# Gating projection of a hybrid encoder layer: x transposed by the host, inner dimension outermost

## The chip, the cores and the metric

The kernel runs on one core of a Trainium2 chip. Its time is the device time of one launch in microseconds; "before" is the median of three runs. A trace of one execution, taken by the profiler, shows what each engine did and when. The engines are TensorE (PE; its weight loads are listed as PEld), VectorE (DVE), ScalarE (ACT), GpSimd (POOL) and SyncE (SP), which here only issues transfers.

## The reference

One layer on x of 1024 rows (sequence) by 1024 columns, all in float32. The change is in its first part:

```python
h = rms_norm(x, norm_mix[l])
proj = h @ w_in[l]                       # 1024 x 2304 columns
z_sgu, z_s5, z_qkv = jnp.split(proj, [2 * SGU_WIDTH, 2 * SGU_WIDTH + S5_WIDTH], axis=-1)
o_a = sgu_mixer(jax.nn.gelu(z_sgu), ...) # 512 columns: u * (w @ rms_norm(v) + b), blocks of 128 rows
o_b = s5_mixer(z_s5, ...)                # 256 columns: a diagonal state-space scan, GELU, GLU
o_c = band_attention(q, k, v, ...)       # 3 x 512 columns: 8 heads, each chunk of 64 sees 9 chunks
x = x + group_rms(concat[o_a, o_b, o_c]) @ w_out[l]
x = x + moe(rms_norm(x))                 # 16 experts, two of one group for each row
```

`sgu_mixer` is called the gating unit here, and the product that gives its 512 columns the gating projection.

## The kernel before

**Precision.** Each large product of float32 operands is made of three matmuls (`mm3`, L129): both operands are split into a high part in a shorter format and a low part that holds the rest (`split`, L125: ScalarE writes the high part, VectorE the low one), and high times high, high times low and low times high are added up in one PSUM bank. A matmul has at most 512 columns here.

**Norm and projections.** The RMS norm's gain `gmix` is folded into the transposed x; its row factor `rs` is applied when a projection's result is copied out of PSUM. For each of four pairs of 128-row tiles of x (loop `pr`, L199), TensorE transposes the pair's 16 squares of 128x128 into PSUM (`hTp`, L205), ScalarE writes the high part `hT` scaled by the gain (L209), VectorE the low part `lT` (L210). ScalarE also squares the rows of x with a sum (L218), from which a short chain of VectorE steps makes `rs` for the pair. Then `sgu_proj` (L190) runs the gating projection of the pair's two tiles: all eight slices of the inner dimension (k) by three matmuls into one bank, and a GELU scaled by `rs` into `gz`.

**What follows.** S5's projection (L439 on, 96 matmuls, result transposed in `zT`), then k's, q's and v's (`qk_proj`, L608, and the loop at L855), eight tiles each of 24 matmuls. Attention, the output product, the router and the experts come after.

**Side work.** The gating unit (`sgu`, L249, six steps) and S5 (`s5`, L459, 21 steps) are generators in a list `side`. `tick(n)` (L90) draws n steps of the first one that isn't finished. The ticks stand beside the projections' tiles: two for each of the four tiles of S5's projection, which use up the gating unit's steps, then one for each tile of k, q and v, for S5's.

```python
    def tick(n=1):
        while n and side:
            try:
                next(side[0])
                n -= 1
            except StopIteration:
                side.pop(0)
```

**Order.** Up to attention, the order in which each engine (and each queue of transfers) gets its instructions isn't written out: a planner simulates the program and gives each engine, whenever it is free in that simulation, the ready instruction that stands earliest in the program. On the chip each engine then works strictly in that order. Attention, output and experts have an order written by hand.

**Memory.** PSUM has eight banks: three buffers of two banks with the tag `big`, and two of one bank with the tag `acc`. In SBUF there are 16 buffers of 4 KB per partition with the tag `slot`, 12 more with the tag `far` (the names in `FAR`, L28, among them `xt`, `bc_in`, `wsr`, `vn`, `vh`), and four with the tag `raw` for weights as they arrive. A tile that finds no free buffer waits until an earlier one is no longer read.

**Transfers.** x and the large weights are loaded by SyncE's queue. The small parameters (`gains`, the gating unit's `row256`, `sgb` and `wsr`, S5's `lam`, `ldt`, `bc_in` and `d5`, and `gqk`, from which VectorE makes `gq` at L635) are loaded by ScalarE's queue.

Of the kernel before, what the change touches and what calls it, by code (L numbers as in the profile page):

```python
# [4 lines left out]
F32 = mybir.dt.float32  # L5
F32R = mybir.dt.float32r
BF = mybir.dt.bfloat16
# [24 lines left out]
def trunk(tc, A, dbg=None, upto="all"):  # L32
# [35 lines left out]
    def slot(name, shape, dt=F32, far=None):  # L68
        far = name in FAR if far is None else far
        return slots.tile(shape, dt, name=name, tag="far" if far else "slot", bufs=FARS if far else SLOTS)  # L70
# [4 lines left out]
    def big(name, shape, dt=F32):  # L75
        return psum.tile(shape, dt, name=name, tag="big", bufs=3)

    def acc(name, shape, dt=F32):
        return psum.tile(shape, dt, name=name, tag="acc", bufs=2)
# [19 lines left out]
    def f32(ap):  # L99
        return ap.bitcast(F32)  # L100
# [37 lines left out]
    def load_x(tb):  # L138
        t = slot("xt", [128, D])
        sp.dma_start(t, x[tb * 128:(tb + 1) * 128, :])  # L140
        return t
# [6 lines left out]
    def junk():  # L148
        return work.tile([128, D], BF, name="junk", tag="w2")
# [17 lines left out]
    def load_w(c0, n, far=()):  # L167

        his, los = [], []
        per = 1024 // n  # L170
        for r in range(KD // per):
            rw = raw("rw", [128, per, n])
            sp.dma_start(rw, w_in[r * per * 128:(r + 1) * per * 128, c0:c0 + n]
                         .rearrange("(k p) c -> p k c", p=128))
            h = slot("wh", [128, per, n], F32R, far=r in far)
            l = slot("wl", [128, per, n], F32R, far=r in far)
            split(h, l, rw)
            his += [h[:, i] for i in range(per)]
            los += [l[:, i] for i in range(per)]
        return his, los  # L180

    def proj(out, sel, w, ks=range(KD)):
        his, los = w
        for k in ks:
            mm3(out, hT[k][:, sel], lT[k][:, sel], his[k], los[k], k == ks[0], k == ks[-1])

    gz = []
    rs = const("rs", [128, NT])

    def sgu_proj(tb):  # L190
        a = acc("pj", [128, 512])
        proj(a, slice(tb * 128, (tb + 1) * 128), W["sgu"])
        if tb % 2 == 0:
            gz.append(slot("gz", [128, 2, 512]))
        act.activation(gz[tb // 2][:, tb % 2], a, AF.Gelu_apprx_tanh, scale=rs[:, tb:tb + 1])

    W = {}
    xs = {0: load_x(0), 1: load_x(1)}
    for pr in range(4):  # L199
        for kq in range(2):  # L200
            p = big("hTp", [128, 4, 256])
            for q in range(2):
                for k in range(4):
                    kk = 4 * kq + k
                    pe.transpose(p[:, k, q * 128:(q + 1) * 128], xs[2 * pr + q][:, kk * 128:(kk + 1) * 128], ident)  # L205
            for k in range(4):
                kk = 4 * kq + k
                sl = slice(pr * 256, (pr + 1) * 256)
                act.activation(hT[kk][:, sl], p[:, k], AF.Copy, scale=gmix[:, kk:kk + 1])  # L209
                dve.scalar_tensor_tensor(lT[kk][:, sl], p[:, k], gmix[:, kk:kk + 1], f32(hT[kk][:, sl]),  # L210
                                         op0=OP.mult, op1=OP.subtract)
        if pr == 0:
            W["sgu"] = load_w(0, 512)
            for tb in range(2, NT):
                xs[tb] = load_x(tb)
        ss = small.tile([128, 2], F32, name="ssx")
        for q in range(2):
            act.activation(junk(), xs[2 * pr + q], AF.Square, accum_out=ss[:, q:q + 1])  # L218
        rsqrt(rs[:, 2 * pr:2 * pr + 2], ss, 2, 1.0 / D)
        if pr == 3:  # L220
            W["s5"] = load_w(512, 256)
        sgu_proj(2 * pr)
        sgu_proj(2 * pr + 1)
    W["k"] = load_w(1280, 512)

    div8, mod8 = const("div8", [128, 16]), const("mod8", [128, 8])
# [10 lines left out]
    row256 = const("row256", [128, 256])  # L237
    gsgu, glub = row256, row256
    wsr = slot("wsr", [128, 4, 128])
    act.dma_start(gsgu, bass.AP(tensor=A["sgu_norm"].tensor, offset=A["sgu_norm"].offset, ap=[[0, 128], [1, 256]]))  # L240
    sgb = const("sgb", [128, 4])
    act.dma_start(sgb, A["sgu_bT"])
    act.dma_start(wsr, A["sgu_wT"])
    pool.memset(wsr[64:128, :, 0:64], 0.0)
    wsh = slot("wsh", [128, 2, 4, 128], F32R)
    split(wsh[:, 0], wsh[:, 1], wsr)
# [58 lines left out]
            v = v.rearrange("p (a b c) -> p a b c", a=shape[1], b=shape[2])  # L305
        return v

    lam = const("lam", [128, 2, NG])
    act.dma_start(lam, A["lam2"])
    ldt = const("ldt", [128, NG])  # L310
    act.dma_start(ldt, bass.AP(tensor=A["log_dt"].tensor, offset=A["log_dt"].offset, ap=[[0, 128], [1, NG]]))
    bc_in = slot("bc_in", [128, 4, NG, 16])
    act.dma_start(bc_in, A["bc2"])
    d5 = const("d5", [16, NG])
    act.dma_start(d5, A["s5_dT"])
    dt = const("dt5", [128, NG])
    act.activation(dt, ldt, AF.Exp)
    th = const("th5", [128, NG])
# [120 lines left out]
    for i in range(2):  # L439
        for ts in (slice(0, 512), slice(512, S)):  # L440
            a = acc("pj", [128, 512])
            his, los = W["s5"]
            for k in range(KD):
                wk, wl_ = (t[:, i * 128:(i + 1) * 128] for t in (his[k], los[k]))
                mm3(a, wk, wl_, hT[k][:, ts], lT[k][:, ts], k == 0, k == KD - 1)
            act.activation(zT[i][:, ts], a, AF.Copy)
            tick(2)
    for i in range(2):
        p = big("s5z", [128, 8, 128])
        for j in range(8):  # L450
# [157 lines left out]
    def qk_proj(name, w):  # L608
        out = []
        for tb in range(NT):  # L610
            a = acc("pj", [128, 512])
            proj(a, slice(tb * 128, (tb + 1) * 128), w)
            if tb % 2 == 0:
                out.append(slot(name, [128, 2, 512]))
                s16 = small.tile([128, 2, 8], F32, name="s16")
                r16 = small.tile([128, 2, 8], F32, name="r16")
            act.activation(out[-1][:, tb % 2], a, AF.Copy, scale=rs[:, tb:tb + 1])
            sq = work.tile([128, 512], F32, name="sqk", tag="w2")
            act.activation(sq, a, AF.Square, scale=rs[:, tb:tb + 1])
            dve.tensor_reduce(s16[:, tb % 2], sq.rearrange("p (h c) -> p h c", c=64), axis=AX.X, op=OP.add)  # L620
            if tb % 2 == 1:
                rsqrt(r16.rearrange("p a b -> p (a b)"), s16.rearrange("p a b -> p (a b)"), 16, 1.0 / 64)
                ov = out[-1].rearrange("p t (h c) -> p t h c", c=64)
                dve.tensor_tensor(ov, ov, bc(r16[:, :, :, None], [128, 2, 8, 64]), op=OP.mult)
            tick(1)
        return out

    kt_ = qk_proj("kt", W["k"])
    W["q"] = load_w(768, 512, (0, 1))
    qt_ = qk_proj("qt", W["q"])  # L630
    W["v"] = load_w(1792, 512, (3,))
    gqk = const("gqk", [128, 2])
    act.dma_start(gqk, A["qk2"])
    gq = const("gq", [128, 1])
    dve.scalar_tensor_tensor(gq, gqk[:, 0:1], 64 ** -0.5, gqk[:, 1:2], op0=OP.mult, op1=OP.mult)  # L635

# [969 lines left out]
def layout(inputs):  # L1606

    import numpy as np
    i = {k: np.asarray(v) for k, v in inputs.items()}
    f = np.ascontiguousarray  # L1610
    o = {"x": i["x"], "w_in": i["w_in"][0]}
    lr, li = i["s5_lambda_re"][0].T, i["s5_lambda_im"][0].T
    o["lam2"] = np.stack([np.concatenate([lr, lr]), np.concatenate([li, li])], 1)
    br, bi = (i[n][0].transpose(1, 0, 2) for n in ("s5_b_re", "s5_b_im"))
    cr, ci = (i[n][0].transpose(2, 0, 1) for n in ("s5_c_re", "s5_c_im"))
    o["bc2"] = np.stack([np.concatenate(p) for p in ((br, bi), (bi, br), (cr, ci), (ci, cr))], 1)
    o["log_dt"] = i["s5_log_dt"][0]
    o["s5_dT"] = i["s5_d"][0].reshape(16, 16).T
    o["glu_w"] = i["s5_glu_w"][0]
    o["glu_b"] = i["s5_glu_b"][0]  # L1620
    o["sgu_norm"] = i["sgu_norm"][0]
    o["sgu_bT"] = i["sgu_b"][0].T
    o["sgu_wT"] = i["sgu_w"][0].transpose(2, 0, 1)
    o["qk2"] = np.stack([np.concatenate([i[n][0]] * 2) for n in ("q_norm", "k_norm")], 1)
    o["norm_ffn"] = i["norm_ffn"][0]
    o["gT"] = np.stack([i[n][0].reshape(8, 128).T for n in ("norm_mix", "out_norm", "norm_ffn")], 1)
    o["w_out"] = i["w_out"][0]
    o["w_router"] = np.concatenate([i["router_group_w"][0], i["router_expert_w"][0].transpose(1, 0, 2).reshape(D, 16)], 1)
    o["b_router"] = np.concatenate([i["router_group_b"][0], i["router_expert_b"][0].reshape(16)])
    o["w_gu"] = np.concatenate([i["w_gate"][0], i["w_up"][0]], 2)  # L1630
    o["w_down"] = i["w_down"][0]
    rb = i["rel_bias"][0]
    rx = np.concatenate([np.repeat(rb[:, 512:], 639 - 255, axis=1), rb[:, 129:512][:, ::-1]], axis=1)

    o["relT"] = np.stack([rx[:, 127 - q:767 - q] for q in range(128)], 1)
    return {k: f(v) for k, v in o.items()}
# [17 lines left out]
```

## Time and profile before

| | |
|---|---|
| median of 3 runs | 825.13 us (822.68 to 826.71) |
| the profiled execution, its own time | 823.16 us |
| its span, first to last instruction | 821.4 us |
| mean granted TensorE clock | 0.980 of full speed |
| TensorE, VectorE, ScalarE, GpSimd busy | 91%, 65%, 49%, 25% |
| front: gating projection up to | 66.2 us |
| S5's projection up to, about | 90.7 us |
| k's, q's and v's projections up to, about | 268 us |
| attention up to, about | 410 us |

The span is what the trace covers; the execution's own time is 1.8 us longer. Busy time counts matmuls that overlap in the pipeline once. The granted clock is the share of full speed that TensorE was given; its two levels are 1.2 and 2.4 GHz.

### The profile page before, as it was taken

How to read it: one execution, taken by the hardware profiler on the slowest of the kernel's cores; microseconds unless marked ns; L12 is line 12 of the kernel's file. 1: busy time of each engine (PE TensorE's matmuls, PEld its weight loads, DVE VectorE, ACT ScalarE, POOL GpSimd, SP SyncE). 2: the span in 40 equal slices, each digit the busy share in tenths (PEclk: the TensorE clock that was granted, in tenths of full speed). 3: DMA queues.
4: the chain of work that ended last, by engine and by line, in shares of the span. 5: the costliest groups of instructions: out<-in, count | busy, mean ns of one | idle time of the engine just before them, and what ended most of it. 6: DMA issues, size and time to landing. Idle time of an engine off the chain costs nothing. (4 is left out here: it accounts for less than half of the span.)

```text
span 821.4 us, 13661 instructions
## 1 busy us (share of the span) xinstructions
PE 749.3 (91%) x5024; PEld 635.3 (77%) x5025; DVE 533.7 (65%) x1266; ACT 401.9 (49%) x752; POOL 202.9 (25%) x235
## 2 busy tenths in 40 slices
PE   5999999899999777899988999958899999999995
PEld 3878788788888667888876888737778788888884
DVE  4875769968534568777965544768675774575541
ACT  6763342312444677777864333423554553464441
POOL 0000224423132431213001211112332353242221
PEclk9999999999999999999999999989999999999998
DMA  8423011222000410001055233385989999899663
GB/s 310 146 57 103 7 15 15 72 46 41 14 1 1 128 28 1 2 26 53 2 186 203 104 120 112 121 293 176 337 263 273 337 351 305 212 310 308 129 156 55
DMA packets 56516, 111.31 MB, mean 136 GB/s; under 512 B 24272, under 2 KB 28880, under 8 KB 56432
## 3 DMA queue, kind: packets, MB, share of 16 engines
q1 hardware_dynamic: 46880, 84.14, 30.6%
q0 software_dynamic: 6480, 23.60, 12.1%
q10 hardware_dynamic: 3072, 2.49, 1.0%
q8 instruction: 47, 0.77, 0.4%
q14 instruction: 37, 0.30, 0.1%
HBM read 90.05 MB, written 20.17 MB: 134 GB/s over the span
## 5 line engine op out<-in xcount | busy, mean ns | idle before, releaser
L130 PE MATMUL pj<-wh,hTh 128*128 128x512 f32 x256 | 103.8, 406 | 0.8 <-ACT hTh L209 0.7
L131 PE MATMUL pj<-wl,hTh 128*128 128x512 f32 x256 | 102.0, 399 | 2.5 <-DVE wl L127 2.4
L132 PE MATMUL pj<-wh,hTl 128*128 128x512 f32 x256 | 100.8, 399 | 0.5 <-DVE hTl L210 0.4
L130 PE MATMUL gup<-gh,hgh 128*128 128x256 f32 x304 | 89.9, 296 | 1.7 <-PEq L1581 0.3
L132 PE MATMUL gup<-gh,hgl 128*128 128x256 f32 x304 | 87.0, 286 | 3.0 <-DVE hgl L1282 3.0
L1325 PE MATMUL yp<-rwd,hh 128*128 128x256 f32 (+1 forms) x264 | 86.1, 465 | 0.0
L131 PE MATMUL gup<-gl,hgh 128*128 128x256 f32 x304 | 86.1, 283 | 0.0
L977 DVE TENSOR_TENSOR gl<-rwg,gh 128x1024 fp32r<-128x1024 f32 x64 | 78.4, 1247 | 6.9 <-ACT gh L972 6.6
L1325 PEld LDWEIGHTS yp<-rwd,hh 128*128 128x128 f32 x264 | 46.8, 194 | 23.7 <-issue 17.8
L972 ACT ACTIVATE gh<-rwg 128x1024 fp32r<-128x1024 f32 x64 | 64.1, 1052 | 1.1 <-DMA rwg<-in_w_gu 0.2
L130 PEld LDWEIGHTS gup<-gh,hgh 128*128 128x128 f32 x304 | 58.1, 191 | 6.1 <-ACT y L1334 5.2
L132 PEld LDWEIGHTS gup<-gh,hgl 128*128 128x128 f32 x304 | 58.1, 191 | 4.4 <-DVE hgl L1282 3.5
L131 PEld LDWEIGHTS pj<-wl,hTh 128*128 128x128 f32 x256 | 48.7, 190 | 13.6 <-DVE wl L127 3.3
L132 PEld LDWEIGHTS pj<-wh,hTl 128*128 128x128 f32 x256 | 48.5, 190 | 13.1 <-DVE hTl L210 1.6
L130 PEld LDWEIGHTS pj<-wh,hTh 128*128 128x128 f32 x256 | 48.6, 190 | 12.9 <-ACT hTh L209 2.4
L131 PEld LDWEIGHTS gup<-gl,hgh 128*128 128x128 f32 x304 | 58.2, 192 | 0.1
L1337 POOL DMA_INDIRECT out<-y,ix x22 | 38.0, 1729 | 80.9 <-ACT y L1334 44.9
L127 DVE TENSOR_TENSOR ptl<-ps,pth 128x640 fp32r<-128x640 f32 (+2 forms) x53 | 39.7, 748 | 20.3 <-ACT pth L126 19.9
L1334 ACT ACTIVATE y<-yp 128x512 f32<-128x512 f32 (+1 forms) x44 | 21.6, 490 | 61.3 <-PE yp L1325 61.3
L130 PE MATMUL po<-pth,v_h 128*64 128x128 f32 x236 | 46.8, 229 | 2.7 <-DVE oc L765 1.8
L1262 POOL DMA_INDIRECT hg<-h2d,ix x22 | 23.7, 1077 | 102.2 <-PE yp L1325 66.5
L126 ACT ACTIVATE pth<-ps 128x640 fp32r<-128x640 f32 (+2 forms) x53 | 34.3, 646 | 25.3 <-PE ps L732 24.6
(391 smaller groups left out, 1968.9 us busy)
## 6 DMA issues: line engine op xcount, KB each, us to landing
rwg<-in_w_gu SPq DMA_DIRECT2D x62, 512.0 KB, 8.6
rwd<-in_w_down SPq DMA_DIRECT2D x32, 512.0 KB, 6.2
rw<-in_w_in SPq DMA_DIRECT2D x18, 512.0 KB, 4.9
xt<-in_x SPq DMA_DIRECT2D x8, 512.0 KB, 9.1
rwo<-in_w_out SPq DMA_DIRECT2D x8, 512.0 KB, 4.5
xr<-in_x SPq DMA_DIRECT2D x8, 512.0 KB, 4.3
out<-x SPq DMA_DIRECT2D x8, 512.0 KB, 2.6
h2d<-h SPq DMA_DIRECT2D x8, 512.0 KB, 2.9
```

The lines of the kernel that those rows point to most:

```text
L126: act.activation(hi, src, AF.Copy)
L127: (eng_lo or dve).tensor_tensor(lo, src, f32(hi), op=OP.subtract)
L130: pe.matmul(out, ah, bh, start=first, stop=False)
L131: pe.matmul(out, ah, bl, start=False, stop=False)
L132: pe.matmul(out, al, bh, start=False, stop=last)
L972: act.activation(pc[1], pc[0], AF.Copy)
L977: eng.tensor_tensor(t, pc[0], f32(pc[1]), op=OP.subtract)
L1262: pool.indirect_dma_start(out=self.hg, out_offset=None, in_=h2d[:, :], in_offset=bass.IndirectOffsetOnAxis(ap=self.ix, axis=0))
L1325: pe.matmul(self.py[nb][0], self.hh[r], self.ex.d[r][:, ns], start=(r == 0), stop=(r == 1))
L1334: act.activation(self.y[:, ns], p, AF.Copy)
L1337: pool.indirect_dma_start(out=out[:, :], out_offset=bass.IndirectOffsetOnAxis(ap=self.ix, axis=0), in_=self.y, in_offset=None, compute_op= ...
```

## The change

The host also hands over x transposed (`xT`, 1024 x 1024). The loop over pairs of tiles, with its transposes, is replaced by a loop over the inner dimension: for each of four blocks `r` it loads 256 rows of the gating projection's weights and two 128-row slices of xT; for each slice k it makes the weights' high and low parts and xT's (`hT`, `lT`, from SBUF now, 512 columns at a time), and adds the slice's 24 matmuls to eight accumulators, one for each tile of 128 rows. These take all eight PSUM banks until the last k. The plain x is still loaded, behind, for the squares; `rs` is made once for all eight tiles, and the eight GELUs follow.

In front of all this stand 44 matmuls of a tile of ones (`some`, bf16, 128x128) into the last accumulator, whose result is overwritten.

The small parameters' transfers move from ScalarE's queue to SyncE's; S5's four stand right behind the projection. `gqk` takes a buffer of the rotating tag `s16`. The ticks beside S5's projection go; k's tiles draw two steps each, so the gating unit's six and ten of S5's are drawn beside k.

```diff
-    xs = {0: load_x(0), 1: load_x(1)}
-    for pr in range(4):
-        for kq in range(2):
-            p = big("hTp", [128, 4, 256])
-            for q in range(2):
-                for k in range(4):
-                    kk = 4 * kq + k
-                    pe.transpose(p[:, k, q * 128:(q + 1) * 128], xs[2 * pr + q][:, kk * 128:(kk + 1) * 128], ident)
...
-        sgu_proj(2 * pr)
-        sgu_proj(2 * pr + 1)
+    pj = [big("pj", [128, 2, 512]) for _ in range(3)]
+    pj = [t[:, i] for t in pj for i in range(2)] + [acc("pj", [128, 512]) for _ in range(2)]
+    some = const("some", [128, 128], BF)
+    pool.memset(some, 1.0)
+    for _ in range(44):
+        pe.matmul(pj[7][:, 0:128], some, some, start=True, stop=True)
+    for r in range(4):
+        rw = raw("rw", [128, 2, 512])
+        sp.dma_start(rw, w_in[r * 256:(r + 1) * 256, 0:512].rearrange("(k p) c -> p k c", p=128))
+        xT = []
+        for k in (2 * r, 2 * r + 1):
+            xT.append(slot("xt", [128, S]))
+            sp.dma_start(xT[-1], A["xT"][k * 128:(k + 1) * 128, :])
+        wh, wl = slot("wh", [128, 2, 512], F32R), slot("wl", [128, 2, 512], F32R)
+        for i in range(2):
+            k = 2 * r + i
+            g = gmix[:, k:k + 1]
+            split(wh[:, i], wl[:, i], rw[:, i])
+            for sl in (slice(0, 512), slice(512, S)):
+                act.activation(hT[k][:, sl], xT[i][:, sl], AF.Copy, scale=g)
+                dve.scalar_tensor_tensor(lT[k][:, sl], xT[i][:, sl], g, f32(hT[k][:, sl]), op0=OP.mult, op1=OP.subtract)
+            for tb in range(NT):
+                sel = slice(tb * 128, (tb + 1) * 128)
+                mm3(pj[tb], hT[k][:, sel], lT[k][:, sel], wh[:, i], wl[:, i], k == 0, k == KD - 1)
+    lam = const("lam", [128, 2, NG])
+    sp.dma_start(lam, A["lam2"])
...
+    ss = const("ssx", [128, NT])
+    for tb in range(NT):
+        act.activation(junk(), load_x(tb), AF.Square, accum_out=ss[:, tb:tb + 1])
+    rsqrt(rs, ss, NT, 1.0 / D)
+    W["s5"] = load_w(512, 256)
+    for tb in range(NT):
+        act.activation(gz[tb // 2][:, tb % 2], pj[tb], AF.Gelu_apprx_tanh, scale=rs[:, tb:tb + 1])
     W["k"] = load_w(1280, 512)
...
-    act.dma_start(wsr, A["sgu_wT"])
+    sp.dma_start(wsr, A["sgu_wT"])
...
             act.activation(zT[i][:, ts], a, AF.Copy)
-            tick(2)
...
-            tick(1)
+            tick(2 if name == "kt" else 1)
...
-    gqk = const("gqk", [128, 2])
-    act.dma_start(gqk, A["qk2"])
+    gqk = small.tile([128, 2], F32, name="gqk", tag="s16")
+    sp.dma_start(gqk, A["qk2"])
...
-    o = {"x": i["x"], "w_in": i["w_in"][0]}
+    o = {"x": i["x"], "xT": i["x"][0].T, "w_in": i["w_in"][0]}
```

## Rows read from the trace of the kernel before

**Rows 1.** Page, busy time of each engine, share of the span, instructions.
```profile
PE 749.3 (91%) x5024; PEld 635.3 (77%) x5025; DVE 533.7 (65%) x1266; ACT 401.9 (49%) x752; POOL 202.9 (25%) x235
```

**Rows 2.** Busy time by stage: length, engines' busy (instructions), granted clock, DMA share, GB/s.
```profile
0.00:9.48 9.48, 0.00 (x1) 0.00 (x1) 0.69 (x8) 4.02 (x6) 1.49 (x17) 1.00 0.69 204
9.48:13.38 3.90, 3.67 (x16) 3.27 (x17) 2.29 (x8) 2.08 (x5) 0.00 (x0) 1.00 1.02 378
...
15.20:66.20 51.00, 50.39 (x238) 40.38 (x239) 40.00 (x135) 38.41 (x65) 0.31 (x1) 1.00 0.36 125
...
67.10:90.70 23.60, 23.58 (x108) 19.40 (x108) 16.83 (x70) 4.23 (x5) 0.00 (x0) 1.00 0.24 86
...
96.50:153.00 56.50, 56.17 (x301) 47.23 (x299) 46.43 (x95) 21.25 (x46) 19.22 (x18) 1.00 0.11 11
...
159.20:162.00 2.80, 2.80 (x9) 2.22 (x10) 2.80 (x4) 0.01 (x1) 0.83 (x1) 0.74 0.84 260
162.00:164.00 2.00, 2.00 (x6) 1.59 (x5) 1.98 (x7) 0.00 (x0) 0.00 (x0) 0.51 0.77 207
164.00:268.00 104.00, 103.92 (x526) 86.80 (x526) 58.90 (x146) 39.46 (x71) 28.61 (x34) 1.00 0.11 21
...
580.00:700.00 120.00, 112.52 (x775) 95.71 (x774) 77.99 (x135) 60.72 (x106) 42.77 (x37) 0.97 0.96 314
```

**Rows 3.** TensorE's waits, all of the span: total, times, longest (us).
```profile
PE hTp L205 <- DVE ident L146: 9.5, 1, 9.5
...
PE pj L131 <- DVE wl L127: 2.4, 1, 2.4
...
PE sgup L130 <- ACT vh L126: 1.9, 1, 1.9
```

**Rows 4.** Timeline, 0 to 10 us: start, duration, engine, line, [idle <- releaser].
```profile
0.75 0.86 SPq L140 DMA_DIRECT2D xt<-in_x  x2
...
4.61 3.20 SPq L173 DMA_DIRECT2D rw<-in_w_in  x4
...
8.93 1.06 ACT L126 ACTIVATE wh<-rw 128x1024 fp32r<-128x1024 f32 x1 [0.27 <-DMA rw<-in_w_in]
9.06 0.16 DVE L635 SCALAR_TENSOR_TENSOR gq<-gqk 128x1 f32<-128x1 f32 x1 [7.91 <-DMA gqk<-in_qk]
...
9.48 3.67 PE L205 MATMUL hTp<-ident,xt 128*128 128x128 f32 x16 [9.48 <-DVE ident L146]
```

**Rows 5.** Timeline of TensorE, transposes at 25.9 us and projection's end.
```profile
25.92 2.78 PE L205 MATMUL hTp<-ident,xt 128*128 128x128 f32 x24
...
61.05 0.40 PE L131 MATMUL pj<-wl,hTh 128*128 128x512 f32 x1
...
65.95 0.39 PE L132 MATMUL pj<-wh,hTl 128*128 128x512 f32 x1
...
67.12 0.50 PE L130 MATMUL pj<-hTh,wh 128*128 128x512 f32 x1 [0.66 <-ACT gz L195]
```

**Rows 6.** Groups by line and shape, ScalarE and VectorE, 0 to 66.2 us.
```profile
L218 ACT ACTIVATE junk<-xt 128x1024 bf16<-128x1024 f32 x8 | 8.4, 1049 | 0.0
L195 ACT ACTIVATE gz<-pj,rs 128x512 f32<-128x512 f32 x7 | 4.7, 686 | 7.8 <-PE pj L132 7.8
...
L126 ACT ACTIVATE wsh<-wsr 128x512 fp32r<-128x512 f32 x1 | 0.7, 662 | 0.0
...
L127 DVE TENSOR_TENSOR wsh<-wsr,wsh 128x512 fp32r<-128x512 f32 x1 | 0.7, 693 | 0.0
```

**Rows 7.** Timeline at 103.7 us, GpSimd and VectorE.
```profile
103.68 1.28 POOL L508 TENSOR_TENSOR cs<-cs,cst 128x512 f32<-128x512 f32 x1 [4.71 <-DVE rq_y L118]
103.72 1.27 DVE L114 SCALAR_TENSOR_TENSOR rq_a<-rq_y,rq_h 128x16 f32<-128x16 f32 x1
```

**Rows 8.** Timeline of TensorE before the experts: matmuls on a bf16 tile.
```profile
551.53 1.91 PE L1472 MATMUL yp<-ohs 128*128 128x512 bf16 x4 [0.22 <-issue]
```

**Rows 9.** Waits of SyncE's DMA queue, 0 to 60 us.
```profile
SPq L432 <- DVE bcm L415: 30.1, 1, 30.1
```

More of the change, by code (lines that the diff above doesn't have):

```diff
@@ L185, in proj @@
             mm3(out, hT[k][:, sel], lT[k][:, sel], his[k], los[k], k == ks[0], k == ks[-1])
-    gz = []
+    gz = [slot("gz", [128, 2, 512]) for _ in range(NT // 2)]
     rs = const("rs", [128, NT])
[L190 to L195, printed above, removed]
-    W = {}
@@ L198, in trunk @@
-    xs = {0: load_x(0), 1: load_x(1)}
-    for pr in range(4):
-        for kq in range(2):
-            p = big("hTp", [128, 4, 256])
-            for q in range(2):
-                for k in range(4):
-                    kk = 4 * kq + k
-                    pe.transpose(p[:, k, q * 128:(q + 1) * 128], xs[2 * pr + q][:, kk * 128:(kk + 1) * 128], ident)
[L206 to L221, printed above, removed]
-        sgu_proj(2 * pr)
-        sgu_proj(2 * pr + 1)
@@ new lines, in trunk @@
+    lam = const("lam", [128, 2, NG])
+    sp.dma_start(lam, A["lam2"])
+    ldt = const("ldt", [128, NG])
+    sp.dma_start(ldt, bass.AP(tensor=A["log_dt"].tensor, offset=A["log_dt"].offset, ap=[[0, 128], [1, NG]]))
+    bc_in = slot("bc_in", [128, 4, NG, 16])
+    sp.dma_start(bc_in, A["bc2"])
+    d5 = const("d5", [16, NG])
+    sp.dma_start(d5, A["s5_dT"])
+    ss = const("ssx", [128, NT])
+    for tb in range(NT):
+        act.activation(junk(), load_x(tb), AF.Square, accum_out=ss[:, tb:tb + 1])
@@ L239, in trunk @@
     wsr = slot("wsr", [128, 4, 128])
-    act.dma_start(gsgu, bass.AP(tensor=A["sgu_norm"].tensor, offset=A["sgu_norm"].offset, ap=[[0, 128], [1, 256]]))
+    sp.dma_start(gsgu, bass.AP(tensor=A["sgu_norm"].tensor, offset=A["sgu_norm"].offset, ap=[[0, 128], [1, 256]]))
     sgb = const("sgb", [128, 4])
-    act.dma_start(sgb, A["sgu_bT"])
-    act.dma_start(wsr, A["sgu_wT"])
+    sp.dma_start(sgb, A["sgu_bT"])
+    sp.dma_start(wsr, A["sgu_wT"])
     pool.memset(wsr[64:128, :, 0:64], 0.0)
@@ L306, in tmp @@
         return v
[L308 to L315, printed above, removed]
     dt = const("dt5", [128, NG])
```

## The prediction

> **What bounds the kernel now.** I read the page first. TensorE is busy for 91% of the span and no other engine for more than 65% [rows 1], so a change pays where TensorE stands idle or does work that need not be done. The table by stage says where that is [rows 2]. TensorE does nothing for the first 9.48 us, then only transposes for 3.90 us; from 15.2 to 66.2 us it is busy for 50.4 of 51.0 us. That is the gating projection. S5's projection follows (67.1 to 90.7 us), then k's (to about 153 us), q's and v's, and from 164 to 268 us TensorE is busy for 103.9 of 104.0 us. The list of waits names the holes [rows 3]: 9.5 us before the first transpose, behind VectorE's `ident` (L146); 1.9 us for the gating unit's `vh`; 2.4 us for the low part of q's weights.
>
> The first hole is not what it seems. `ident` needs an iota only. But VectorE works in the order in which the planner emitted its instructions, and ahead of `ident` it put `gq` (L635), which waited 7.91 us for the tiny transfer `gqk` [rows 4]. A planned order that trusts a late transfer stops everything behind it; the change has to be read with that in mind.
>
> **The change, part by part.**
>
> *No transposes.* Sixty-four 128-column transposes leave TensorE, and with them the wait for `ident`. Before, the projection's last matmul gives way at 65.95 + 0.23 = 66.18 us [rows 5]. That is made up of 9.48 us idle, 3.90 us with the first 16 transposes, 48 later ones at 2.78/24 = 0.116 us (5.6 us) [rows 5], 192 matmuls at (65.95 - 61.05)/21 = 0.233 us (22 matmuls lie between those two rows, both counted), so 44.8 us, and 2.4 us of small waits and slow clock: 66.2 us.
>
> *When the new projection starts.* It needs the first weights, the first 128 rows of x transposed, one ScalarE split of a 128x512 piece, one scaled copy and one VectorE subtraction. SyncE's first transfer is issued at 0.75 us [rows 4]. Weights issued at 4.61 us were there at 8.93 us, 4.3 us later [rows 4]; so the first 512 KB land at about 5.1 us. xT's first 512 KB lie right behind them on the queue: at 378 GB/s [rows 2] 1.4 us more, 6.5 us. The weights' split is over by then. The scaled copy costs 0.66 us and the subtraction 0.69 us [rows 6] (the two split rows of 128x512), and the first matmul waits for the copy alone: 7.2 us. I allow 0.4 us for the third matmul, which needs the subtraction. Bounds: 5.8 us, if both transfers land together 4.3 us after the first issue; 10.1 us, if the second takes its own 4.3 us behind the first.
>
> *Whether it keeps up.* Each k step is 24 matmuls, 5.6 us. ScalarE needs 3 x 0.66 = 2.0 us for it and VectorE 3 x 0.69 = 2.1 us [rows 6]. Twelve transfers of 512 KB at 378 GB/s take 16.6 us, so the eighth xT lands near 5.1 + 11 x 1.4 = 20 us and is needed at 46 us. TensorE sets the pace: end at 7.2 + 0.4 + 44.8 = 52.4 us, 13.8 us earlier.
>
> *Matmuls on ones.* They wait only for a memset. Four 512-column bf16 matmuls after an idle stretch took 1.91 us [rows 8], about 0.12 us per 128 columns with the tail; 44 take about 5 us and are over near 6.5 us, under the cover of the transfers. Bounds: the slow transposes' pace, 3.67/16 = 0.229 us [rows 4], gives 10.1 us and would delay the start by 4 us; the fast pace of 0.116 us gives 5.1 us. What they buy is the clock: the first 16 transposes ran at half the later ones' pace, 3.67 us against 1.86. I have priced the first real matmuls at full speed, so this gain is in the 13.8 us; if the pause between the last one on ones and the first real one lets the clock fall, some 1.8 us are lost again.
>
> *The squares and the gate.* All eight GELUs now wait for one `rs`, so for all eight plain x tiles, 4 MB behind the 6 MB in front. At 378 GB/s all 10 MB take 28 us, plus half a megabyte for `bc_in`: x is there by about 35 us. The squares, 8 x 1.05 = 8.4 us [rows 6] and their short readouts, find room on ScalarE, which the k steps use for 16 of 45 us. Cost nothing; if x were late, all eight GELUs (8 x 0.69 = 5.5 us [rows 6]) would stand in front of S5's projection.
>
> *All eight PSUM banks.* The projection holds them to its end, and S5's projection needs one back. The GELUs follow the matmuls of the last k step (0.7 us per tile against 0.69 us [rows 6]), so the wait is one GELU, as before: 0.66 us [rows 5]. No change.
>
> *The gating unit beside k.* Its 24 matmuls leave S5's projection, and with them the 1.9 us wait [rows 3]: minus 1.9 us; the matmuls themselves only move. Bounds: 0, if a wait of that size returns beside k. VectorE and ScalarE keep the same work, but in k's stretch VectorE is already busy for 46.4 of 56.5 us [rows 2], and two ticks per k tile draw two more S5 steps ahead of the split of q's weights. The waits there were 2.4 us plus a half-speed clock after it (0.74 and 0.51 in the next 4.8 us [rows 2]), about 1.7 us lost. I charge 1 us more for the extra steps, between a gain of 4.1 us (both vanish) and a loss of 8 us (below).
>
> *Transfers moved from ScalarE's queue to SyncE's.* Eight small ones now stand behind the 6 MB; their users are S5's preparation and the gate, needed after 52 us. `gqk` leaves VectorE's head. Cost nothing, since VectorE has over 20 us to spare in the projection. What it costs if the planner puts one user early is a rival below.
>
> Sum: -13.8 - 1.9 + 1.0 = -14.7 us. The profiled execution took 823.16 us, span 821.4; so 808.5. It lies 2.0 us under the median of 825.13, so on the scale of the runs **810.5 us**. Nothing after v's projection depends on absolute time: attention and experts are set off by the work before them.
>
> **Rivals.**
>
> *VectorE becomes the bound beside k (818 us).* If half of the gating unit's VectorE work, of the 16.8 us it and its neighbours do in S5's stretch [rows 2], lands in k's, 46.4 + 8 + two S5 steps fill the 56.5 us, and the 8 us come out in front of q. For it: with GpSimd running, a VectorE step of 16 elements took 1.27 us beside a 1.28 us GpSimd one [rows 7], and S5's steps use GpSimd much. Against it: what needs only the GELUs can still run during S5's projection. The Trainium skill ("SBUF — State Buffer", SBUF: two separate sides) says that VectorE with two SBUF inputs and GpSimd share a port that one holds for its whole instruction while the other waits. By that rule every such overlap would cost VectorE a whole GpSimd instruction; the trace agrees in the pair just named.
>
> *A queue's head blocks (slower, 831 us).* SyncE's queue stood 30.1 us behind L432, which waited for VectorE [rows 9]. Should the planner put the last plain x tiles behind that transfer, the last lands near 35 + 30 = 65 us, and its square (1.05 us), `rs` (eleven short VectorE steps, some 2 us) and all GELUs (5.5 us) come after: S5's projection starts near 74 us instead of 67.1 us, 7 us later than before; with -1.9 and +1 that is 6 us more. It turns the sign once the last x lands after about 59 us. For it: the planner did the like with `gqk`. Against it: the x loads stand ahead of L432 in the program, and their buffers come free with the first k steps.
>
> *The gain doesn't reach the end (825 us).* From 580 to 700 us the DMA engines are busy for 0.96 of the time [rows 2]. If the weights' stream set the pace by an absolute start, the front would not count. Against it: those loads wait for buffers that the same stage frees, and TensorE is busy for 112.5 of 120 us there.
>
> **How the numbers follow.** Forecast (803 to 816) 0.68; VectorE bound (816 to 820) 0.16; gain absorbed 0.06; queue blocked 0.05; the waits near q also vanish and the start is early (802 or a little less) 0.05. Range: downwards 1.4 us (early start) + 1 + 4.1 us give 804, and 2 us of scatter between runs 802; upwards the 8 us and the runs' scatter give 820. A measurement here tells 0.5%, some 4 us, from no change: faster 0.89, same 0.06, slower 0.05.
>
> **What would show it.** Right: no transposes named hTp; the first matmul on xT's product near 7 us; the last of the gating projection near 52 us; no 1.9 us wait for `vh`; k's first tile some 15 us earlier; the same shift at attention's start. Wrong: waits on DMA in the first 20 us; GELUs that start after 55 us; more than 5 us of waits on VectorE in front of q; or a shift that shrinks between 164 us and the end.

## The result, and the profile after

The change makes the kernel slower: 832.28 us in the median of 11 runs (829.26 to 835.66) against 825.13 of the kernel before (821.93 to 828.86), a ratio of 1.0086 with a 95% interval of 1.0061 to 1.0111. The forecast was 810.5, with 802 to 820 as its range. The profiled execution took 829.26 us, its span is 827.5.

The front came nearly as forecast. TensorE's timeline at its start and at the end of the gating projection (start, duration, engine, line, names and shapes, [idle <- releaser]; compare [rows 4, 5]):

```profile
7.07 0.79 PE L130 MATMUL pj<-wh,hTh 128*128 128x512 f32 x1 [7.07 <-ACT hTh L209]
7.67 0.63 PE L131 MATMUL pj<-wl,hTh 128*128 128x512 f32 x1
8.09 0.63 PE L132 MATMUL pj<-wh,hTl 128*128 128x512 f32 x1
8.52 3.47 PE L195 MATMUL pj<-some 128*128 128x128 bf16 x44
11.80 0.48 PE L130 MATMUL pj<-wh,hTh 128*128 128x512 f32 x1
...
54.94 0.40 PE L132 MATMUL pj<-wh,hTl 128*128 128x512 f32 x1
55.89 0.39 PE L237 MATMUL rsp<-mod,rsx 128*128 128x8 f32 x2 [0.55 <-ACT gz L228]
56.53 0.50 PE L130 MATMUL pj<-hTh,wh 128*128 128x512 f32 x1 [0.26 <-DVE r L239]
```

S5's projection starts at 56.53 us, 10.6 us earlier than before [rows 5]. The first real matmul is at 7.07 us. But the 44 matmuls on ones don't stand in front of it: they come behind the third real matmul and take 3.3 us of time in which operands were there.

ScalarE copies out the first tile of k and the first tile of q at these times; first the kernel before, then the changed one:

```profile
102.74 0.80 ACT L617 ACTIVATE kt<-pj,rs 128x512 f32<-128x512 f32 x1
...
167.54 0.69 ACT L617 ACTIVATE qt<-pj,rs 128x512 f32<-128x512 f32 x1 [8.33 <-PE pj L132]
```

```profile
86.64 0.69 ACT L613 ACTIVATE kt<-pj,rs 128x512 f32<-128x512 f32 x1 [2.31 <-PE pj L132]
...
177.99 0.69 ACT L613 ACTIVATE qt<-pj,rs 128x512 f32<-128x512 f32 x1 [0.26 <-PE pj L132]
```

k starts 16.1 us earlier and q 10.5 us later: the stretch between the two is 26.6 us longer. Of that, 4.6 us are given back by the end of v (its last copy is 5.8 us later), and that shift reaches the end: the span is 6.1 us longer. So the loss has one place. Busy time in just this stretch, from k's first copy to q's, before and after (columns as in [rows 2]: length, PE, PEld, DVE, ACT, POOL, granted clock, DMA share, GB/s):

```profile
102.74:167.54 64.80, 61.48 (x323) 51.59 (x322) 54.70 (x103) 20.59 (x37) 22.56 (x18) 0.97 0.22 43
```

```profile
86.64:177.99 91.35, 74.65 (x392) 62.84 (x391) 81.61 (x180) 27.39 (x45) 41.68 (x31) 0.89 0.19 35
```

VectorE has 26.9 us more to do here, and the stretch is 26.6 us longer. By its rows, S5's lines take some 41 us of VectorE for 27 before (ten of S5's steps are drawn beside k, for eight before); most of the rest of the increase is the gating unit's. Not all of the 26.6 us is idle time of TensorE: it stands idle for 16.7 us, for 3.3 before, and is busy for 13.2 us longer, with 69 more matmuls (the gating unit's 24, 3.8 us, and S5's) and at a lower clock. By slices of 10 us, VectorE is full from 110 to 170 us; TensorE has idle time from 120 us on, and the granted clock falls to 0.66 and 0.52 of full speed (0.5 is the lower of its two levels):

```profile
120.00:130.00 10.00, 8.06 (x43) 6.45 (x41) 10.00 (x25) 3.69 (x7) 3.50 (x3) 1.00 0.28 26
130.00:140.00 10.00, 7.00 (x30) 6.41 (x31) 9.93 (x16) 0.51 (x1) 7.65 (x7) 0.66 0.12 13
...
150.00:160.00 10.00, 5.89 (x50) 5.54 (x50) 9.97 (x15) 2.44 (x5) 9.15 (x6) 1.00 0.19 48
160.00:170.00 10.00, 3.61 (x11) 2.60 (x12) 9.88 (x19) 1.40 (x2) 3.45 (x3) 0.52 0.50 89
170.00:180.00 10.00, 10.00 (x40) 8.29 (x39) 5.53 (x6) 2.41 (x5) 5.86 (x5) 0.79 0.57 127
```

What TensorE waits for in the stretch are S5's operands, which VectorE and GpSimd make (waits of TensorE: total, times, longest):

```profile
PE s5y L542 <- POOL f L523: 6.0, 2, 5.7
PE s5y L542 <- DVE w L532: 3.8, 1, 3.8
PE s5a L479 <- DVE rq_a L116: 2.7, 1, 2.7
PE s5y L542 <- DVE w L534: 2.3, 3, 1.1
```

TensorE works in order, so k's matmuls behind such a one wait with it. Earlier, VectorE is late for another reason. Four of its rows, and one of ScalarE:

```profile
33.60 0.17 DVE L109 TENSOR_SCALAR rq_h<-ssx 128x8 f32<-128x8 f32 x1 [9.65 <-ACT junk L224]
45.51 0.69 DVE L127 TENSOR_TENSOR wsh<-wsr,wsh 128x512 fp32r<-128x512 f32 x1 [6.42 <-ACT wsh L126]
...
73.39 1.67 DVE L268 SCALAR_TENSOR_TENSOR vn<-gz,rv,row 128x256 f32<-128x256 f32 x4
...
87.94 0.69 DVE L616 TENSOR_REDUCE s<-sqk 128x8 f32<-128x512 f32 x1 [12.88 <-ACT sqk L615]
```

```profile
87.80 1.06 ACT L126 ACTIVATE vh<-vn 128x1024 fp32r<-128x1024 f32 x1
```

VectorE stands 9.65 us behind the eight squares and 6.42 us behind the gating unit's weights, with S5's preparation queued behind both; the gating unit starts at 69.71 us instead of at the last GELU, 56 us. Then `vn` is done at 75.1 us, but the planner put `vh` behind k's first copies. In that pause VectorE is idle for 12.88 us.

### The profile page after: what moved, and what is told of

It reads as the page before. It is cut to its first block, busy times and chain, and to the rows that moved or that the text cites. A ratio compares the mean times of both kernels' runs of the same rounds, so it can differ in the third digit from the quotient of the medians.

```text
span 827.5 us, 13580 instructions
## 1 busy us (share of the span) xinstructions
PE 748.0 (90%) x5004; PEld 634.6 (77%) x5005; DVE 525.9 (64%) x1221; ACT 399.6 (48%) x739; POOL 207.2 (25%) x236
## 5 line engine op out<-in xcount | busy, mean ns | idle before, releaser
L728 PE MATMUL ps<-ident,st 128*128 128x128 f32 x240 | 38.2, 287 | 9.6 <-ACT st L719 8.8
```

The costliest lines, as they stand in the source:

```text
L728: pe.transpose(pp[:, b], st[:, b * 128:(b + 1) * 128], ident)
```

## The experiments

Theory after the result: the new places of the side steps put the gating unit and two S5 steps per tile beside k, VectorE becomes the bound there, and the front's gain is lost. Rival A: the new front delays S5's preparation, and with it everything, wherever the steps stand. Rival B: the ones. Rival C: it is the gating unit beside k, not S5's steps. All kernels were timed in five rounds; those of one group ran on one chip with the kernel before beside them (825.0, 826.8, 824.6, 826.0 and 826.0 us in the five groups). The planner lays out each variant's order anew, so an edit can move more than it names.

| run | us | ratio to before, 95% interval |
|---|---|---|
| changed kernel | 832.3 | 1.0086 (1.0061 to 1.0111) |
| e1 side steps as before | 824.4 | 0.9995 (0.9976 to 1.0014) |
| e2 steps back beside S5's projection only | 835.0 | 1.0122 (1.0092 to 1.0151) |
| e3 one step beside k only | 831.1 | 1.0068 (1.0045 to 1.0091) |
| e5 ones in front | 835.5 | 1.0126 (1.0103 to 1.0149) |
| e8 e1 + small transfers early | 815.1 | 0.9872 (0.9853 to 0.9892) |
| e9 e1 + S5's preparation early | 816.5 | 0.9881 (0.9845 to 0.9918) |
| e11 e1 + both + ones in front | 810.8 | 0.9829 (0.9803 to 0.9855) |
| e12 preparation early, new steps | 831.9 | 1.0062 (1.0045 to 1.0079) |
| e16 kernel before + new steps alone | 843.0 | 1.0208 (1.0188 to 1.0228) |
| e14 e9 with two steps per tile of k | 829.4 | 1.0068 (1.0042 to 1.0095) |
| e15 e9 without steps beside S5's projection | 834.5 | 1.0111 (1.0085 to 1.0136) |
| e13 changed kernel, S5's GpSimd work on VectorE | 828.0 | 1.0043 (1.0027 to 1.0059) |
| e18 e16, S5's GpSimd work on VectorE | 839.0 | 1.0152 (1.0121 to 1.0183) |
| e19 before, S5's GpSimd work on VectorE | 824.0 | 0.9975 (0.9953 to 0.9997) |
| e17 e11, S5's GpSimd work on VectorE | 810.6 | 0.9810 (0.9784 to 0.9835) |
| e20 e11 without ones | 817.6 | 0.9905 (0.9875 to 0.9934) |
| e6 e1 with ones in front | 830.0 | 1.0058 (1.0033 to 1.0083) |

### First: the side steps, and the ones

```diff
             act.activation(zT[i][:, ts], a, AF.Copy)
+            tick(2)
...
-            tick(2 if name == "kt" else 1)
+            tick(1)
```

e1 makes both edits, e2 the first alone, e3 the second alone. e5 makes this one alone:

```diff
-    pool.memset(some, 1.0)
+    dve.memset(some, 1.0)
```

> The changed kernel with the side steps issued as before the change: two behind each of the four blocks of S5's projection, one behind each tile of k. Theory (the order of the side steps: the gating unit and two S5 steps a tile fall beside k, VectorE becomes the bound there, TensorE waits for S5's operands): the loss of some 26 us between the first tile of k and the first of q goes, the front's gain stays, 806 to 816 us, VectorE under 95% busy in 120 to 170 us. Rival A (the new front leaves S5's preparation on VectorE late, so the gating unit is late wherever its steps are issued): 822 to 834 us, and the gap from the last tile of k to the first of q stays near 30 us. Rival B (the placing of the 44 matmuls on ones): unchanged, 829 to 835 us.

> The changed kernel with only the two side steps behind each block of S5's projection put back; k's tiles keep two each. Theory (VectorE's total beside k is what counts): six steps of the gating unit leave the stretch beside k and six more of S5 enter it, so VectorE is still full there, 822 to 836 us. Rival C (it is the gating unit beside k that costs): 806 to 818 us. Rival A (late preparation in the front): 822 to 834 us, with the gating unit's matmuls as late as in the changed kernel.

> The changed kernel with one side step behind each tile of k in place of two; S5's projection has none, as in the changed kernel. Theory: beside k lie six steps of the gating unit and two of S5, the rest falls beside q and v, VectorE is no longer full beside k, 810 to 820 us. Rival C (the gating unit beside k costs): 826 to 834 us. Rival A (late preparation): 824 to 834 us.

> The changed kernel with the tile of ones set by VectorE in place of GpSimd, which lets the 44 matmuls on ones be placed ahead of the first real matmul. They then run before the first operands arrive at 7.07 us and not from 8.52 to 11.80. Theory (the loss is in the order of the side steps): the front's end moves by 3 to 4 us and at most that arrives at the end, 828 to 832 us. Rival B (the front was the larger loss): 815 to 822 us.

e1 lies between the theory and rival A. The stretch from k's first copy to q's is as the theory had it (64.3 us, before the change 64.8), but the time is rival A's: 7.9 us are won at the end, where the theory expected 16 or more. What is missing is a new hole in e1, seen in TensorE's waits and in two slices:

```profile
PE sgup L130 <- ACT vh L126: 9.1, 2, 7.8
```

```profile
70.00:80.00 10.00, 8.69 (x44) 6.92 (x43) 6.76 (x27) 1.06 (x1) 0.00 (x0) 1.00 0.01 2
80.00:90.00 10.00, 2.22 (x10) 1.50 (x8) 8.78 (x41) 2.40 (x3) 0.00 (x0) 0.76 0.01 3
```

With the steps back in S5's projection, TensorE meets the gating unit's matmuls there, and they aren't ready: the 1.9 us wait of before [rows 3] has become 9.1 us. So rival A holds for a second loss. e2 fell in the theory's range, e3 in the rivals'; e5 missed both ranges, and rival B, which wanted 815 to 822 us, falls. Bringing the ones in front starts the GELUs 4.2 us earlier (47.1 against 51.2 us) and yet ends 3 us later (1.0126 against 1.0086; the intervals just touch). The earlier front has another planned order, in which S5's first copy `zT` stands in ScalarE's queue behind S5's preparation:

```profile
PE pj L130 <- ACT zT L443: 5.7, 1, 5.7
```

### Second: S5's preparation

e8 is e1 with the transfers `gsgu`, `sgb` and `wsr` moved up to stand behind `d5`, ahead of x's eight. e9 is e1 with the lines of S5's preparation moved up:

```diff
+    xs = [load_x(tb) for tb in range(NT)]
+    carve = {"t": slot("s5c", [128, 1024]), "o": 0}
...
     for tb in range(NT):
-        act.activation(junk(), load_x(tb), AF.Square, accum_out=ss[:, tb:tb + 1])
+        act.activation(junk(), xs[tb], AF.Square, accum_out=ss[:, tb:tb + 1])
```

e11 has both moves and the ones set by VectorE. e12 is e9 with the changed kernel's steps.

> The changed kernel with the side steps as before the change (as the run with ticks as before, 824.4 us), and the transfers of the gating unit's gain, bias and weights moved ahead of x's eight. Theory (S5's preparation on VectorE, held by in-order waits for these weights and for the squares, delays the gating unit, and that is the hole of 9 us at 78 to 90 us): VectorE is busy with the preparation in 24 to 45 us, the hole closes, 812 to 818 us. Rival (the hole comes from the gating projection's steps being issued where they are, whatever the preparation): 822 to 827 us, hole unchanged.

> The changed kernel with the side steps as before the change, the transfers left where the change has them, and S5's preparation written ahead of the squares of x, so that VectorE does it from 24 us on and not behind them. Theory: as for the earlier transfers, 812 to 818 us, the gating unit starts within 2 us of the last GELU. Rival: 822 to 827 us.

> The changed kernel with the side steps as before the change, the small transfers and S5's preparation early, and the ones set by VectorE so that the matmuls on them run ahead of the first real one. Theory: the front's gain of some 13 us over the kernel before arrives at the end but for 1 or 2 us, 808 to 815 us. Rival (S5's steps beside k and q take whatever the front gives): 818 to 826 us.

> The changed kernel, its side steps as the change has them, with S5's preparation written ahead of the squares. Theory (two separate losses, the larger the steps beside k): VectorE stays full in 110 to 170 us and TensorE waits there, 822 to 831 us. Rival (the late preparation alone made the backlog beside k): 808 to 818 us.

The times of e8, e9 and e11 came out as the theory had them, e12 0.9 us above its range. One sign failed: in e9 the gating unit was to start within 2 us of the last GELU, and starts 6 us behind it (63.4 us), since splits of k's weights stand before it on VectorE (in e8 5.5 us). In e8 the gating unit starts at 61.60 us and TensorE's wait for it is back to its old size:

```profile
PE sgup L130 <- ACT vh L126: 2.0, 1, 2.0
```

e11 is 1.7% faster than the kernel before, and faster than both kernels of the case. Its front, with the ones where they were meant to be:

```profile
1.06 4.87 PE L195 MATMUL pj<-some 128*128 128x128 bf16 x44 [1.06 <-DVE some L193]
6.67 0.50 PE L130 MATMUL pj<-wh,hTh 128*128 128x512 f32 x1 [0.74 <-ACT hTh L209]
7.01 0.39 PE L131 MATMUL pj<-wl,hTh 128*128 128x512 f32 x1
...
52.11 0.51 PE L130 MATMUL pj<-hTh,wh 128*128 128x512 f32 x1 [0.26 <-DVE r L383]
```

S5's projection starts at 52.11 us, 15.0 us earlier than before, and its span (807.9) is 13.5 us shorter. e12 shows the two losses as separate, and not as additive: with the new steps, mending the preparation buys nothing measurable (1.0062 against 1.0086, the intervals overlap), since TensorE doesn't meet the late gating unit until k.

### Third: the steps alone, and their halves

> The kernel before with one part of the change alone: no side steps behind the blocks of S5's projection, two behind each tile of k. Theory (the steps' places cost by themselves, whatever the front): slower than before by about the 15 us that they cost in front of the same early preparation, 834 to 845 us, VectorE full in 120 to 180 us and TensorE waiting for S5's operands there. Rival (they cost only together with the new front): 823 to 829 us.

> The changed kernel with S5's preparation written ahead of the squares and two side steps behind each block of S5's projection (the run with the preparation early, 816.5 us), but two steps behind each tile of k in place of one. Theory (how many S5 steps stand behind each tile of k decides): 824 to 836 us. Rival C (the gating unit beside k is what costs): 813 to 819 us.

> The same base, with no side steps behind the blocks of S5's projection and one behind each tile of k. Theory (steps per tile decide): k's stretch is light, the rest of S5 falls beside q and v, 814 to 822 us. Rival C (the gating unit beside k costs): 826 to 834 us.

e16 is the kernel before with nothing but `tick(2)` gone from S5's projection and `tick(2 if name == "kt" else 1)` beside k. It is 2.1% slower, 18 us, more than the whole change. From k's first copy to q's:

```profile
96.94:188.21 91.27, 76.33 (x392) 64.37 (x391) 81.58 (x180) 26.10 (x45) 42.56 (x31) 0.89 0.20 35
```

VectorE's 81.58 us are the changed kernel's 81.61, and the length is the same within 0.1 us: this loss in the stretch doesn't depend on the front. In time, the parts don't simply multiply up. Steps alone (e16, 1.0208) and the new front alone (e1, 0.9995) would make 1.0203, and the change has 1.0086. With the preparation early (e9, 0.9881) they would make 1.0087, and e12 has 1.0062: there the product fits within the intervals. So under the new steps the late preparation is hidden.

Of the halves, e14 came out as the theory had it; e15 missed by 12 us, close to rival C's range. On this front either half alone costs at least as much as both (e12). The two lose in different places. With two steps per tile of k (e14) TensorE waits beside k for S5's operands, 6.0 us for `w` and 2.7 us for `f`. With one, and none beside S5's projection (e15), k and q are not held up: v's last copy stands at 258.1 us, 6.6 us earlier than in e9. But its span is 15.3 us longer, so 22 us are lost behind v: S5's last steps, its GLU and norm, are left over for the start of attention. The GLU's 32 matmuls, done before v's end in e9, now stand there and take 9.5 us of TensorE; TensorE also waits for these steps, and from 250 to 290 us it is busy for 25.3 us, in e9 for 33.4. Four of e15's waits, from 236 to 310 us, that e9 doesn't have; the first is attention's own:

```profile
PE po L759 <- ACT ocT L753: 4.5, 1, 4.5
PE glu L581 <- ACT yT L576: 4.1, 2, 3.0
...
PE oTbp L771 <- POOL y L600: 1.9, 1, 1.9
...
PE yTp L574 <- DVE sg L583: 0.9, 1, 0.9
```

e3 shows the same on the other front: v's last copy is 22.4 us earlier than in the changed kernel, the same waits stand behind it, and the time is the changed kernel's within some 1 us. Rival C so falls too: it is not the gating unit beside k that loses time in e15. Of the places tried, the old ones are those where VectorE gets through in every stage.

### Fourth: is it the sharing with GpSimd?

In the changed kernel small VectorE steps and GpSimd's own stretch each other beside k:

```profile
155.16 4.74 POOL L531 TENSOR_TENSOR w<-ak,bcm 128x512 f32<-128x512 f32 x1
155.16 0.67 DVE L469 TENSOR_TENSOR w1t<-ak,bcm 128x512 f32<-128x512 f32 x1
...
155.84 1.20 DVE L127 TENSOR_TENSOR wl<-rw,wh 128x1024 fp32r<-128x1024 f32 x1
...
157.74 1.21 DVE L127 TENSOR_TENSOR wl<-rw,wh 128x1024 fp32r<-128x1024 f32 x1
158.88 1.04 DVE L118 SCALAR_TENSOR_TENSOR rq_y<-rq_a,rq_y 128x16 f32<-128x16 f32 x1
```

The GpSimd product of this line took 1.06 us at 105.98 us of the kernel before; here it takes 4.74 beside a run of VectorE products. The Trainium skill ("SBUF — State Buffer", SBUF: two separate sides) has the port that the two share go to whichever starts first, for its whole instruction. The trace agrees that one stands while the other works: here GpSimd is held up, in [rows 7] VectorE, and so is the last step above, whose 16 elements take 1.04 us and end with GpSimd's product at 159.9 us. But GpSimd's 3.7 us beyond its 1.06 span several VectorE instructions, not one. To price the sharing, seven lines of S5 (L470, L502 to L505, L523, L531) go from GpSimd to VectorE, for instance:

```diff
-            pool.tensor_tensor(w2[:, 1], ai, p4, op=OP.mult)
+            dve.tensor_tensor(w2[:, 1], ai, p4, op=OP.mult)
```

> The changed kernel with GpSimd's 28 products and sums of S5 done by VectorE. Adds about 28 x 0.68 = 19 us to VectorE, which is full beside k; takes away what GpSimd's work stretches there, by the rows about 17 us (small steps 1.0 us in place of 0.17, products 1.2 in place of 0.68, GpSimd's own 4.74 in place of 1.06). Theory (the sharing between VectorE and GpSimd makes most of the loss): within 6 us of the changed kernel's 832, the small steps at 0.17 us throughout. Rival (it is VectorE's own amount of work): 843 to 855 us.

> The kernel before with the new places of the side steps alone (the run of 842.95 us), and GpSimd's 28 products and sums of S5 done by VectorE. If the sharing between VectorE and GpSimd makes the steps' loss of 18 us, it falls to within 6 us of the kernel before with the same move to VectorE. If the order and the amount of VectorE's work make it, it stays more than 10 us above that kernel.

> The kernel before with GpSimd's 28 products and sums of S5 done by VectorE, its order of steps as it is. VectorE gets some 19 us more work and loses what GpSimd stretches: 820 to 832 us by either theory; it is the measure for the run beside it.

> The mended version of the change (side steps as before the change, early preparation and transfers, ones in front; 810.8 us) with GpSimd's 28 products and sums of S5 done by VectorE. If the sharing costs in this order too, 800 to 809 us; if VectorE's own work does, 812 to 825 us.

e13 fell where the sharing was to make the loss, but that test can't separate: VectorE's extra work and the stretching it removes cancel. e18 and e19 do separate. Without GpSimd the new steps still cost 1.0152 against 0.9975, 1.8%, some 15 of the 18 us; the other 3 us are within the intervals. From k's first copy to q's, e19 and e18 have next to no sharing left, and the new steps lengthen this stretch by 23.0 us, where they did by 26.5 with GpSimd at work (64.80 and 91.27 us). VectorE is busy for 77.81 of e18's 86.23 us:

```profile
102.88:166.09 63.21, 60.32 (x318) 50.65 (x317) 52.12 (x123) 20.51 (x37) 0.23 (x2) 0.97 0.20 39
```

```profile
96.54:182.77 86.23, 73.52 (x386) 61.71 (x385) 77.81 (x206) 25.57 (x42) 2.68 (x5) 0.88 0.20 37
```

So the sharing isn't the cause, or a small part of it at most; the place of VectorE's work is. e17 is no faster than e11 (810.6 us, between its two ranges): in the old places the sharing costs nothing that could be won this way.

### Fifth: what the ones are worth

e20 is e11 without the ones; e6 is e1 with the edit of e5.

> The mended version (810.8 us) without the 44 matmuls on ones. In the changed kernel the first three real matmuls, with nothing ahead of them on TensorE, ended 0.42 us apart, and those behind the ones 0.23 us apart. If the ones are what brings that, the first 5 us or so of real matmuls run at the slower pace and some 2 us are lost: 811 to 814 us. If they are not needed, 809 to 811 us.

> The changed kernel with the side steps as before the change (824.4 us) and the ones in front, the preparation of S5 left late. Theory (the late preparation, not the front's end, decides when the gating unit and S5's projection are through): the 3.5 us that the ones give back in front are lost in a longer hole, 821 to 829 us. Rival (the front's end decides): 818 to 821 us.

Without the ones, the second to the seventh real matmul start 0.42 to 0.43 us apart and those from the eighth on 0.23 (e20's TensorE); in e11 the pace is 0.23 us from the second on. The granted clock reads 1.00 in the first 10 us of both traces, so what the prediction calls buying the clock shows in the pace alone:

```profile
6.91 0.80 PE L130 MATMUL pj<-wh,hTh 128*128 128x512 f32 x1 [6.91 <-ACT hTh L205]
7.51 0.63 PE L131 MATMUL pj<-wl,hTh 128*128 128x512 f32 x1
7.93 0.63 PE L132 MATMUL pj<-wh,hTl 128*128 128x512 f32 x1
...
9.64 0.50 PE L130 MATMUL pj<-wh,hTh 128*128 128x512 f32 x1
9.98 0.40 PE L131 MATMUL pj<-wl,hTh 128*128 128x512 f32 x1
10.21 0.40 PE L132 MATMUL pj<-wh,hTl 128*128 128x512 f32 x1
```

The GELUs start 2.3 us later than in e11, about the expected 2 us. The end is some 6 us later (0.9905 against 0.9829), more than expected. By the traces it is 4.6 us later at k's first copy (93.1 against 88.5 us) and 5.4 at v's last; TensorE's wait for `vh` in e20 is 2.8 us against 2.0, with a granted clock of 0.83 in 80 to 90 us where e11 has 1.00. What makes up the rest stays open. e6 is another miss, by 1 us: 5 us slower than e1 with a front that is 3.8 us earlier. Its waits hold both holes, 10.0 us for `vh` and 5.7 us for `zT`. Until S5's preparation is early, an earlier front isn't an earlier end.

## Why the prediction was wrong

*The step that failed* is the last part of the sum, the gating unit beside k: charged 1.0 us, with 8 us as its bound. It measured 26.6 us between k's first copy and q's. Of these, 4.6 came back up to v's last copy, and 3.8 are the gating unit's matmuls, which the prediction rightly had as only moved; some 18 us are left, and e16 shows the steps alone at 18 us of time. Mechanism and place were named, as the rival "VectorE becomes the bound beside k", but its price and the argument against it were wrong. By the rival's own sum, 46.4 + 8 of 56.5 us, the work would have fitted, so the 8 us didn't follow from it. "What needs only the GELUs can still run during S5's projection" would have been a fact of the program; what counts is the planned order. `vn` did run there, but `vh` was emitted behind k's first copies, and VectorE stood idle with the gating unit unfinished. Most of that unit's VectorE work then fell beside k, together with ten of S5's steps for eight: 26.9 us more in that stretch, where 54.70 of 64.80 us were taken already. About 10 us were free, and the prediction had shown as much from [rows 2]: 46.4 of 56.5. That room was to be compared with all the VectorE work drawn there, not with half of one window's. The room didn't even get used: VectorE idles for 9.7 us of the longer stretch too, 6.1 of them before 110 us, where it waits in order for k's squares and for TensorE. Why the planner placed `vh` so late with ScalarE idle from 75.1 to 79.2 us stays open.

*The ones* were costed as "over near 6.5 us, under the cover of the transfers". Their bound, if they delay the start, was 4 us; they cost 3.3, because the planner held them back for a memset that stands behind an iota on GpSimd; with the memset on VectorE (e5, e11) they stand in front. On the chip the GpSimd memset was done at 1.23 us. The prediction had met the like with `gqk` [rows 4] and didn't apply it.

*The squares and the moved transfers* were costed at nothing, the squares since ScalarE has room, the transfers since "VectorE has over 20 us to spare in the projection". It has; but it spent 16 us of that in two in-order waits, 9.65 for the squares and 6.42 for `wsr`. The room was used up by waiting. Under the new steps this cost nothing that shows (e12); with the old ones it is some 9 us (e1 against e8). "Needed after 52 us" was true of the gating unit and false of the split at the head of VectorE's order. The weights `wsr` themselves came late, since on SyncE's queue they stand behind six weight loads (issued from 23.41 us on) and were issued at 39.69 us.

*Right:* the start (7.07 us, forecast 7.2), TensorE's pace (no wait from 11.80 us to the end), the end but for the ones (S5 starts 10.6 us earlier; 15.0 in e11), the GELUs close behind the matmuls, the vanished wait for `vh` (0.6 us for 1.9), and that nothing after v depends on absolute time: 5.8 us at v's last copy, 6.1 at the end. A queue blocked for the plain x and the gain absorbed by the weights' stream didn't occur. With the steps in their old places, the preparation and the small transfers early and the ones in front (e11), the time is 810.8 us (808.95 to 815.66), which was forecast for the change. That it fits to 0.3 us is luck: e11's front gains 15.0 us for the 13.8 of the sum, and its wait for `vh`, which the sum took out, is still 2.0 us.

## What to carry to other kernels

When side work is moved between stages, add up, for each engine and stage, what the stage has and what is drawn into it, and compare with the stage's length: an engine with 10 us of room that gets 27 us becomes the bound, however idle it is over the whole kernel (VectorE here: 65%). Room beside the work counts only as far as the order lets it be used; ask of every instruction that now waits for something later what stands behind it on its engine. And test an edit of the front together with what follows: here an earlier front gave a later end until the work behind it was freed.

## What the runs showed of the hardware

In the old places of the steps, moving 28 products and sums from GpSimd to VectorE (e19) left VectorE no busier: 529.5 us over the whole span, against 533.7 [rows 1]. From 96.5 to 153 us, where sixteen of the 28 lie, it was busy for 44.42 us, against 46.43 with GpSimd at work [rows 2], and the kernel was 0.25% faster (interval 0.03 to 0.47). What GpSimd took off VectorE there it gave back in stretched VectorE steps: twelve of 128x16 took 396 ns each before and 167 in e19.

```profile
96.50:153.00 56.50, 56.30 (x302) 47.26 (x300) 44.42 (x112) 21.15 (x47) 0.23 (x2) 1.00 0.11 11
```
